# A second group of six gated tiles as block products in the down projection of a hybrid encoder trunk

## The chip, the core and the metric

The kernel runs as one program on one core of a Trainium2 chip. The metric is the device time of one execution in microseconds (us), given as the median of several runs; one further execution is taken by the hardware profiler, and every view in this document comes from such a profiled execution. TensorE (PE) multiplies matrices into PSUM, VectorE (DVE) and ScalarE (ACT) read PSUM and do arithmetic on SBUF, GpSimd (POOL) issues DMAs here that add to their destination in DRAM, and SyncE (SP) issues the plain loads.

## What is computed

Two layers of a streaming encoder on 1040 tokens (16 learned ones and 1024 of input) of width 1024. Each layer has an attention part, which the change leaves alone, and a gated feed-forward part with 2816 = 22 x 128 inner features:

```python
def conv_ffn(x, w_up, conv_w, conv_b, w_down):
    h = x @ w_up
    L = h.shape[1]
    hp = jnp.pad(h, ((0, 0), (CONV_W - 1, 0), (0, 0)))
    hc = conv_b
    for j in range(CONV_W):
        hc = hc + hp[:, j:j + L] * conv_w[j]
    u, g = jnp.split(hc, 2, axis=-1)
    return (jax.nn.silu(g) * u) @ w_down

for i in range(DEPTH):
    ...
    h = h + conv_ffn(rms_norm(h, ffn_norm[i]), w_up[i], conv_w[i], conv_b[i], w_down[i])
return rms_norm(h, final_norm)[:, N_META:]
```

The change concerns the last product, with `w_down`, and the addition to the residual `h`.

## The kernel before

**Layout.** Features lie on the 128 partitions and tokens along the free axis. The result of a layer's feed-forward part is 8 output tiles `m` of 128 features by 1040 tokens (1024 in the last layer, which drops the learned tokens). The 22 tiles that the down projection sums over are the gated tiles `j`, each 128 inner features. The tokens are worked in two halves of 520 (512 in the last layer), each in two matmul columns of 260 (256).

**Precision.** Every operand is split into a high and a low part (ACT casts, DVE subtracts: `weights`, `up_split`, `split`), and `mm3` (L253 to L255) multiplies high by high, low by high and high by low: three matmuls for each product of tiles.

**The order of the down projection.** `GROUPS` lists, per layer, groups of gated tiles as (kind, first tile, number of tiles); `LAST` holds the three last tiles. Before the change: three tiles of kind "n", eight of kind "s", two groups of four of kind "r", then `LAST`.

- Kinds "n" and "r" are plain (`plain` inside `ffn_down`): for each of the 8 output tiles and 2 halves, the group's tiles are accumulated in one of four PSUM places of two banks each. For "r", the residual tile `h` has been loaded from DRAM (`load_residual`, L1542) and DVE adds the PSUM sum onto it in SBUF (L1567). For "n", ACT copies the sum into one of three tiles `do` (L1569), and POOL issues a DMA that adds `do` to the residual in DRAM, `hm` (L1571).
- Kind "s" is done by seven block products in place of eight (`down_blocks`): the group's tiles are cut into two halves, output tiles are taken in pairs, and tokens in halves, which gives a two-by-two block product. Its left operands are sums and differences of weight blocks (`block_operand`, L1065 loads, L1075 combines), its right operands `X` are sums and differences of gated tiles. The four pairs are worked in a fixed order of products; the sums leave PSUM by copies (L1474) and adds (L1473) into tiles `du` and `dg`, which two accumulating DMAs for each pair add to `hm` (L1494, L1498).
- `LAST` is done by `down_last`, in column chunks of 400, 384 and 256 tokens (512, 256 and 256 in the last layer) over eight single PSUM banks. It adds the sum to the residual `h` in SBUF and feeds the next norm. Its weights stay in SBUF in tiles `wl`.

**The operands.** The gated tiles come back from DRAM (`actd`). `prepare` is one generator that goes through the groups in order and, step by step, loads tiles (L1365 for "s", L1359 for the others), splits plain tiles into `ah` and `al` and builds the operands of an "s" group: seven splits and four combinations (L1413) for each run of two tiles per half, or of one where the number is odd. Its steps are taken by `pump` at fixed points of the loops, as far as SBUF slots are free, and by `complete` where they are needed at once. SBUF slots of 1040 elements are lent out of one list, 39 of them in this stage; an "s" group of eight tiles holds 28 for its operands, and gives them back product by product while the last pair of output tiles is worked.

**What sets the order.** PE runs in the order of the program. The instructions of the other engines and queues are ordered by a planner, which takes the earliest instruction of the program that it thinks ready; each engine and each queue then works strictly in that order, so an instruction that waits holds up those behind it.

Of the kernel before, what the change touches and what calls it, by code (L numbers as in the profile page):

```python
# [46 lines left out]

GROUPS, LAST = (("n", 0, 3), ("s", 3, 8), ("r", 11, 4), ("r", 15, 4)), (19, 3)  # L50
HALVES, HALVES_LAST, HALVES_OUT = (0, 520, 520), (8, 524, 516), (16, 528, 512)
AHEAD = 4
FIRST_OPS = {2: 2, 7: 5}
# [1769 lines left out]
```

## Time and profile before

| | before |
|---|---|
| median of 3 runs | 2519.89 us (2518.92 to 2520.88) |
| profiled execution | 2519.71 us |
| its span | 2517.9 us |
| instructions | 48454 |
| granted TensorE clock, mean over the span | 0.997 |
| DMA | 258.25 MB, mean 103 GB/s |
| accumulating and other DMAs issued by POOL (q0) | 72.68 MB, 10.3% of the 16 engines' span |
| loads issued by SP (q1) | 181.74 MB, 23.2% |

The span is what the profile covers; 1.8 us of the execution lie around it. The down projection of layer 0 takes from 1017 to 1260 us of the span, that of layer 1 from 2263 us to the end, with the final norm. A view that groups instructions gives for each line, engine, operation and tile the shape, the count, the busy time and the mean of one in ns, and behind the bar the idle time of the engine just before them with what ended it. In a list by time each row begins with start and duration. An instruction "h<-down" writes h and reads down.

### The profile page before, as it was taken

To read this page: it belongs to the slowest core of one execution; us is meant where nothing else is said; L and a number is where in the kernel's file an instruction comes from. 1 tells how busy PE (TensorE), PEld (TensorE's weight loads), DVE (VectorE), ACT (ScalarE), POOL (GpSimd) and SP (SyncE) were. 2 spreads that over 40 slices of the span, in tenths; PEclk is the share of its full clock that TensorE was granted. 3 is DMA by queue.
4 is the path that set the end of the run, shared out by engine and by line. 5 is a ranking of instruction groups with operands and counts; after the bars stand their busy time and mean duration, and the time that the engine had idled before them with its cause. 6 is when DMAs were issued, how large, how long until landed. Compare 5 with 4: busy or idle time off the path is not lost.

```text
span 2517.9 us, 48454 instructions
## 1 busy us (share of the span) xinstructions
PE 2468.1 (98%) x19266; PEld 2410.1 (96%) x19266; DVE 1731.1 (69%) x3367; ACT 1283.1 (51%) x2604; POOL 405.6 (16%) x582
## 2 busy tenths in 40 slices
PE   8999999999999999999999999999999999999998
PEld 7989999899999999999999899999999999999997
DVE  7656766769877777853565666777697777787445
ACT  7336666656544455631353466665564444455312
POOL 4033333210000000100211334331100000001002
PEclk9999999999999999999999999999999999999999
DMA  3232134342322224863312222253432222257622
GB/s 123 64 95 63 50 96 131 115 140 72 118 81 81 81 77 132 204 164 115 103 55 70 74 75 77 65 154 109 136 93 92 85 77 80 80 164 176 197 62 77
DMA packets 116211, 258.25 MB, mean 103 GB/s; under 512 B 14624, under 2 KB 31296, under 8 KB 115984
## 3 DMA queue, kind: packets, MB, share of 16 engines
q1 hardware_dynamic: 92832, 181.74, 23.2%
q0 software_dynamic: 22432, 72.68, 10.3%
q8 instruction: 151, 2.47, 0.4%
q10 hardware_dynamic: 720, 0.74, 0.1%
q14 instruction: 76, 0.62, 0.1%
HBM read 174.50 MB, written 67.81 MB: 96 GB/s over the span
## 4 chain that ended last, share of the span: by engine, by line
PE 63%; issue 17%; DVE 12%; ACT 3%; DMA 3%; POOL 1%; SPq 0%; DVEq 0%; POOLq 0%; ACTq 0%
PE mm L253 7%; PE mm L255 7%; PE mm L254 7%; PE up L253 5%; PE up L255 5%; PE up L254 5%; PE down L254 4%; PE down L255 4%; PE down L253 4%; PE av L768 3%; PE tr L750 2%; PE S L714 1%; PE S L713 1%; PE wo L253 1%; PE wo L255 1%
## 5 line engine op out<-in xcount | busy, mean ns | idle before, releaser
L253 PE MATMUL up<-x,hi 128*128 128x260 f32 (+1 forms) x2464 | 697.4, 283 | 2.2 <-DVE hg L1295 1.3
L255 PE MATMUL up<-x,hi 128*128 128x260 f32 (+1 forms) x2464 | 695.5, 282 | 2.4 <-DVE x L1117 2.4
L254 PE MATMUL up<-x,lo 128*128 128x260 f32 (+1 forms) x2464 | 696.1, 283 | 0.3 <-DVE lo L1093 0.3
L255 PEld LDWEIGHTS up<-x,hi 128*128 128x128 f32 x2464 | 465.7, 189 | 3.2 <-DVE x L1117 3.2
L253 PEld LDWEIGHTS up<-x,hi 128*128 128x128 f32 x2464 | 464.6, 189 | 3.3 <-DVE hg L1295 1.8
L254 PEld LDWEIGHTS up<-x,lo 128*128 128x128 f32 x2464 | 464.9, 189 | 0.6 <-DVE lo L1093 0.5
L1093 DVE TENSOR_TENSOR lo<-raw,hi 128x512 fp32r<-128x512 f32 x364 | 247.9, 685 | 187.3 <-ACT hi L1092 179.6
L253 PE MATMUL mm<-xh,hi 128*128 128x348 f32 (+4 forms) x1056 | 362.6, 343 | 0.0
L255 PE MATMUL mm<-xl,hi 128*128 128x348 f32 (+4 forms) x1056 | 339.9, 322 | 0.0
L254 PE MATMUL mm<-xh,lo 128*128 128x348 f32 (+4 forms) x1056 | 338.9, 321 | 0.0
L1092 ACT CAST hi<-raw 128x512 fp32r<-128x512 f32 x364 | 224.5, 621 | 145.1 <-PE up L255 84.1
L253 PEld LDWEIGHTS mm<-xh,hi 128*128 128x128 f32 x1056 | 199.6, 189 | 5.8 <-issue 4.6
L254 PEld LDWEIGHTS mm<-xh,lo 128*128 128x128 f32 x1056 | 199.5, 189 | 0.6 <-issue 0.3
L255 PEld LDWEIGHTS mm<-xl,hi 128*128 128x128 f32 x1056 | 198.4, 188 | 0.6 <-issue 0.3
L253 PE MATMUL down<-ah,hi 128*128 128x260 f32 (+1 forms) x704 | 198.0, 281 | 0.8 <-DVE h L1567 0.8
L254 PE MATMUL down<-ah,lo 128*128 128x260 f32 (+1 forms) x704 | 198.2, 282 | 0.5 <-DVE lo L222 0.4
L255 PE MATMUL down<-al,hi 128*128 128x260 f32 (+1 forms) x704 | 198.4, 282 | 0.0
L379 DVE TENSOR_TENSOR PT<-tr,PT 116x464 fp32r<-116x464 f32 (+3 forms) x240 | 122.2, 515 | 68.9 <-ACT PT L378 67.1
L220 ACT CAST hi<-raw 128x512 fp32r<-128x512 f32 (+1 forms) x160 | 96.8, 607 | 128.7 <-PE down L255 95.1
L729 ACT ACTIVATE P<-P,m 116x924 f32<-116x924 f32 (+4 forms) x144 | 110.6, 768 | 72.1 <-DVE m L721 66.7
L1320 POOL DMA_DIRECT2D actd<-cv x44 | 23.6, 536 | 765.7 <-DVE cv L1319 744.7
L750 PE MATMUL tr<-ident,P 116*116 116x116 f32 x704 | 142.8, 267 | 0.8 <-DVE PT L379 0.5
(302 smaller groups left out, 5766.3 us busy)
## 6 DMA issues: line engine op xcount, KB each, us to landing
raw<-in_wm_dram SPq DMA_DIRECT2D x322, 256.0 KB, 2.8
raw<-in_wd_dram SPq DMA_DIRECT2D x64, 256.0 KB, 3.5
actd<-cv POOLq DMA_DIRECT2D x22, 520.0 KB, 3.0
actd<-cv POOLq DMA_DIRECT2D x22, 512.0 KB, 3.2
cb<-cd SPq DMA_DIRECT2D x16, 520.0 KB, 4.1
st<-actd SPq DMA_DIRECT2D x14, 520.0 KB, 4.6
st<-actd SPq DMA_DIRECT2D x14, 512.0 KB, 4.8
kA<-kA SPq DMA_DIRECT2D x24, 260.0 KB, 4.3
```

The costliest lines, as they stand in the source:

```text
L220: nc.scalar.copy(hi[:, :n, :], raw[:, :n, :])
L253: nc.tensor.matmul(ps, wh, xh[:, c0:c0 + n], start=first, stop=False, skip_group_check=more)
L254: nc.tensor.matmul(ps, wl, xh[:, c0:c0 + n], start=False, stop=False, skip_group_check=more)
L255: nc.tensor.matmul(ps, wh, xl[:, c0:c0 + n], start=False, stop=last, skip_group_check=more)
L379: nc.vector.tensor_tensor(out=lo, in0=src, in1=hi.bitcast(F32), op=ALU.subtract)
L713: nc.tensor.matmul(S[:rows, :n], q["qA"][e][:, qs], q["kA"][e][:, c0:k1], start=True, stop=False)
L714: nc.tensor.matmul(S[:rows, :n], q["qA"][e][:, qs], q["kL"][e][:, c0:k1], start=False, stop=True)
L729: nc.scalar.activation(x, x, AF.Exp, scale=-1.0, bias=low, accum_out=(den if nch < 3 else d2[:rows, 0:1]))
L750: nc.tensor.transpose(tr[:w, j, :rows], P[:rows, o:o + w], id_)
L768: nc.tensor.matmul(av[:, a:width], w.rearrange("p a b -> p (a b)"), x, start=(t == 0 and i == 0), stop=(t == last and i == 1))
L1092: nc.scalar.copy(hi[:, :nk, :], src[:, :nk, :])
L1093: nc.vector.tensor_tensor(out=lo[:, :nk, :], in0=src[:, :nk, :], in1=hi[:, :nk, :].bitcast(F32), op=ALU.subtract)
```

## The change

Behind the first "s" group, the two "r" groups of four gated tiles go. In their place come a plain group of kind "n" with two tiles (11 and 12) and a second "s" group with six tiles (13 to 18), three in each half. With no "r" group left, no sum is added to the residual in SBUF before `LAST`: all of them go to `hm` in DRAM by accumulating DMAs, and `load_residual()` at the end of `ffn_down`'s `run` loads all eight residual tiles, after the last group in program order. `prepare`, `down_blocks` and the dictionary `X` of operands follow the list. No line moves.

```diff
-GROUPS, LAST = (("n", 0, 3), ("s", 3, 8), ("r", 11, 4), ("r", 15, 4)), (19, 3)
+GROUPS, LAST = (("n", 0, 3), ("s", 3, 8), ("n", 11, 2), ("s", 13, 6)), (19, 3)
```

The functions that follow from it, in the lines that decide:

```python
for kind, g0, ng in GROUPS:
    if kind == "s":
        parts.append((g0, ng))
        continue
    ...
        if not isinstance(part, list):
            complete(lambda: built(part))
            blocks[1]()
            continue
...
load_residual()
complete(lambda: all(j in acts for j in range(LAST[0], sum(LAST))))
return hT
```

## The prediction

> **What bounds the kernel now.** I read the page's engine shares first, then its chain that ended last:
>
> ```profile
> PE 2468.1 (98%) x19266; PEld 2410.1 (96%) x19266; DVE 1731.1 (69%) x3367; ACT 1283.1 (51%) x2604; POOL 405.6 (16%) x582
> PE 63%; issue 17%; DVE 12%; ACT 3%; DMA 3%; POOL 1%; SPq 0%; DVEq 0%; POOLq 0%; ACTq 0%
> ```
>
> TensorE is busy for 98% of the span and leads the chain, so a matmul taken out can pay, if nothing else becomes late at its place. To read that place I took the time-ordered list of PE and looked for the instruction that opens each group of the down projection (layer 0 first, then layer 1):
>
> ```profile
> 1017.37 0.28 PE L253 MATMUL down<-ah,hi 128*128 128x260 f32 x1
> 1052.15 0.28 PE L253 MATMUL down<-x,hi 128*128 128x260 f32 x1
> 1134.42 0.28 PE L253 MATMUL down<-ah,hi 128*128 128x260 f32 x1
> 1226.25 0.34 PE L253 MATMUL mm<-ah,wl 128*128 128x400 f32 x1
> 1226.43 0.34 PE L254 MATMUL mm<-ah,wl 128*128 128x400 f32 x1
> 2379.30 0.28 PE L253 MATMUL down<-ah,hi 128*128 128x256 f32 x1
> 2471.29 0.39 PE L253 MATMUL mm<-ah,wl 128*128 128x512 f32 x1
> ```
>
> Layer 0: three plain tiles from 1017.37, the block group from 1052.15, the two plain groups that go straight into the residual ("r") from 1134.42, the last three tiles from 1226.25. The busy times of exactly these stretches (columns: length, PE, PEld, DVE, ACT, POOL, granted clock, DMA share, GB/s):
>
> ```profile
> 1017.37:1052.15 34.78, 34.70 (x290) 34.50 (x289) 33.06 (x38) 26.99 (x41) 6.56 (x8) 1.00 0.85 180
> 1134.42:1226.25 91.83, 91.83 (x770) 91.83 (x769) 35.56 (x53) 14.38 (x24) 1.69 (x2) 1.00 0.33 95
> 1226.25:1260.53 34.28, 34.28 (x220) 34.23 (x219) 26.61 (x46) 20.05 (x42) 17.43 (x17) 1.00 0.40 137
> 2379.30:2471.29 91.99, 91.20 (x770) 91.00 (x769) 34.49 (x51) 13.53 (x22) 1.69 (x2) 1.00 0.30 83
> ```
>
> The replaced "r" stretch is pure TensorE: no gap in layer 0, 0.8 us in layer 1, VectorE at 39%, ScalarE at 16%, clock 1.00. Nothing but matmuls is to be won there, and there is spare time on both evacuating engines.
>
> **What is removed.** By the loops a plain tile costs 8 output tiles x 2 halves x 2 columns x 3 = 96 matmuls. The 8 "r" tiles are 768 matmuls in 91.83 us: 0.1196 us each. After the change two plain tiles cost 192, and six as blocks cost 4 pairs x 7 products x 3 x 2 x 3 = 504: 696 together. Saved: 72 matmuls, 8.6 us a layer, **17.2 us** in two layers. The new plain group lasts 192 x 0.1196 = 23.0 us (2.87 a output tile), a block product 18 x 0.1196 = 2.15 us (24 x 0.1196 = 2.87 in the present group).
>
> **Arithmetic added on VectorE and ScalarE.** Groups by line and shape:
>
> ```profile
> L378 ACT CAST x<-st 128x1040 fp32r<-128x1040 f32 x9 | 9.4, 1066 | 4.1 <-DVE st L1413 3.1 <-DMA st<-actd 0.8
> L379 DVE TENSOR_TENSOR x<-st,x 128x1040 fp32r<-128x1040 f32 x9 | 10.9, 1235 | 1.3 <-ACT x L378 1.2
> L1569 ACT COPY do<-down 128x520 f32<-128x520 f32 x16 | 9.1, 591 | 0.0
> L1473 DVE TENSOR_TENSOR du<-down,du 128x520 f32<-128x520 f32 x8 | 5.6, 697 | 6.8 <-PE down L255 6.8
> L220 ACT CAST hi<-raw 128x384 fp32r<-128x384 f32 x6 | 3.1, 516 | 0.0
> L222 DVE TENSOR_TENSOR lo<-raw,hi 128x384 fp32r<-128x384 f32 x6 | 3.3, 550 | 0.0
> L235 ACT CAST both<-raw 128x256 fp32r<-128x256 f32 x1 | 0.4, 406 | 5.1 <-PE down L255 5.1
> L236 DVE TENSOR_TENSOR both<-raw,both 128x256 fp32r<-128x256 f32 x1 | 0.4, 414 | 0.0
> ```
>
> Per layer, the new operands are 7 splits and 4 combinations, once 1040 and once 520 wide: VectorE 11 x (1.235 + 0.697) = 21.3, ScalarE 7 x (1.066 + 0.591) = 11.6. The two plain tiles' splits: 2.5 and 2.1. Block weights (384 wide): VectorE 28 splits and 16 combinations x 0.550 = 24.2, ScalarE 28 x 0.516 = 14.4. Plain weights (256 wide) 8 x 0.41 = 3.3 on each. Block sums leave by 12 adds x 0.697 = 8.4 and 16 copies x 0.591 = 9.5, plain sums by 16 copies = 9.5. Together 59.7 on VectorE and 50.4 on ScalarE; what goes is less than the 35.56 and 14.38 above. The stretch is now 83.3 us of PE, and some of the operand work falls in the block group before it, so at most 72% and 61%: hidden behind the matmuls. The first plain stretch shows that this works even at 33.06 of 34.78 us on VectorE, with PE busy for 34.70. If that cover failed, the extra 24 us of VectorE a layer would show. The peak is the new plain group: ScalarE 9.5 + 3.3, two wide and seven narrow operand casts (6.3) and four block weights (2.1), 21.2 us in 23.0.
>
> The operands' order I followed through the code: the free slots let five of the seven pairs be built during the last pair of the first block group, as its own operands are given back, and the remainder during the first five plain output tiles. So the second block group finds them ready; bound, if not: the 520-wide half, 11 x 0.697 = 7.7 us a layer. I take 0 here.
>
> **Transfers and waits added.** Plain sums no longer meet the residual in SBUF; 16 accumulating DMAs a layer take them to DRAM.
>
> ```profile
> hm<-do POOLq DMA_DIRECT2D x8, 520.0 KB, 6.3
> h<-hm SPq DMA_DIRECT2D x8, 520.0 KB, 6.2
> raw<-in_wd_dram SPq DMA_DIRECT2D x32, 192.0 KB, 2.4
> q0 software_dynamic: 1148, 4.26, 65.5%
> DMA to landing us min/median/max: 5.2/6.0/10.0
> L1542 SPq EVENT_SEMAPHORE  x16: 17/28/8500, 1124.0 to 2389.1; - x16
> ```
>
> The fourth row is the queue in the 38 us from 1018: 65.5% of all engines for 4.26 MB, eight such DMAs, so 24.9 / 8 = 3.1 us of all sixteen each (the fifth is their time to landing; the last row's three figures are the shortest, median and longest wait of SP in ns).
>
> (a) New plain group: eight of them need 25 us of DMA in 23.0 us. There are three "do" tiles, so the copy of tile m+3 (ScalarE) waits for the landing of tile m: it is wanted 2 x 2.87 + 1.4 = 7.2 us after m ends, and landing takes 0.6 + 6.2 = 6.8. It just fits; at the longest landing, 10.0, it is 3.4 late. Behind a waiting copy on ScalarE stand weight and operand casts, and for these TensorE waits; four PSUM places cover some 4 us. Bounds 0 to 5 us a layer (the early plain group, with 4.3 us a tile, lost 0.1 in layer 0); I take **0.8**, near the row's median.
>
> The Trainium skill, "DMA: Bandwidth & Descriptors" (section Issuing engines are not separate DMA queues), says that all engines' DMAs share the same 16 DMA engines, which is against this change. The section Anatomy of one DMA fits 2.0 us + bytes / 436e3; estimated from it, 520 KB take 3.2 us, the copies would not wait and the sum would be 1.6 us better. The trace's 6.3 us disagrees with the fit for accumulating DMAs.
>
> (b) Blocks: the present block groups show what short products cost when an evacuation is late:
>
> ```profile
> PE down L253 <- ACT dg L1474: 1.0, 1, 1.0
> PE down L253 <- DVE dg L1473: 0.8, 1, 0.8
> PE down L253 <- DVE h L1567: 0.8, 1, 0.8
> PE down L253 <- DVE dg L1473: 0.2, 1, 0.2
> ```
>
> The first and fourth row stand in both layers, the second in layer 1: 1.2 and 2.0 us (28 products each). Another 28 products, each with 0.72 us less to hide an evacuation, beside lighter DMA: bounds 0 to 28 x 0.3 = 8; I take **1.6** a layer. The third row, 0.8 in layer 1, belongs to the removed adds and goes.
>
> (c) Residual loaded last: h6 and h7 can only be read when the last pair's two accumulates have landed, and these start when the last product ends (t0). Today the same chain stands ahead of 92 us of "r":
>
> ```profile
> 1134.59 0.85 POOL L1498 DMA_DIRECT2D hm<-du  x1 [17.14 <-DVE du L1473]
> 1135.51 0.84 POOL L1494 DMA_DIRECT2D hm<-dg  x1
> 1143.16 3.19 SPq L1542 DMA_DIRECT2D h<-hm  x2
> 1073.87 0.33 SPq L211 DMA_DIRECT2D raw<-in_wd_dram  x1
> ```
>
> SP stood for 8.5 us (its semaphore row above) and loaded h6 at 1143.2, 8.8 after the group's end; with 6.2 us of landing h6 comes at t0 + 15, h7 near t0 + 18. TensorE reaches output tiles 6 and 7 of its first column chunk at t0 + 10 and 12 (9 matmuls x 0.18 us a tile), and has eight banks: it goes on for 13 us without any evacuation. VectorE waits some 4 us, and at 26.61 of 34.28 us it has 7.7 to catch up. The last group's weights are issued on SP too, but the fourth row shows SP issuing weights 60 us before the plain group that they serve, so I expect them ahead of the waiting loads. Bounds 0 to 15 us; I take **0.8**.
>
> Sum: -17.2 - 0.8 + 2 x (0.8 + 1.6 + 0.8) = -11.6. The profiled execution took 2519.71 (span 2517.9 and 1.8 around it); 2508.1 follows, and beside the median 2519.89, 0.18 higher, **2508.3 us**.
>
> **The rivals.**
> 1. Waits nearly vanish (as in the "r" stretch): 2519.9 - 17.2 = 2502.7, or 2501 if present block waits shrink too. Against it: every block group so far lost over 1 us. 10%.
> 2. The new plain group is paced by DMA and the short products wait: (a) and (b) near their ends, 3 + 4 us a layer: 2519.9 - 18.0 + 14 = 2516. For it: 25 us of accumulates in 23.0 us, DMA share 0.85 already in the slower group. Against: the cover of four PSUM places. 17%.
> 3. Slower: the last group's weights stand behind the h6/h7 loads on SP. TensorE then stops at t0 until accumulate (8.8 after t0), weight landing (2.4) and both splits (1.1) are over: 12 us a layer, 2519.9 - 18.0 + 24 = 2526. It decides from the point where these waits pass 9 us a layer. For it: SP really did block in front of a row of weight loads. Against: the early issue shown above. 13%. The Trainium skill, "TensorE: Matmul & The Clock Gate" (section What's actually happening), adds that an idle window of about 3.4 us halves the clock; by it some 1.7 us more a stop. In the rows here the clock is 1.00 throughout, and no gap is that long.
> 4. The change is not what it says: the matmul count would stay 19266. Under 1%, in the forecast's share.
>
> **The numbers.** Forecast 60% (2503 to 2513), rivals as above. Without the worst of the third and the best of the first the range is 2501 to 2520. A measurement here tells 0.2%, 5 us, from no change. Faster by more: forecast, rival 1 and a quarter of rival 2, 0.74; within: most of rival 2 and a little of rival 3, 0.14; slower 0.12.
>
> **What would show it.** PE at 19122 matmuls; no "h<-down" adds; 64 "do" copies; 32 accumulates from "do" and 32 from "du"/"dg". The stretch from the first block group's end to the last group's first matmul near 85.7 us (83.3 + 2.4) where it was 91.8. Step (a) is wrong if ScalarE's copies wait on "hm<-do" and PE shows gaps there; (b) if PE's waits on "dg"/"du" in the second block group are far from 1.6; (c) if PE waits for "wl" or "h" after it. I would be wrong altogether if a weight load is issued late because SP waits.

## The result, and the profile after

The changed kernel takes **2545.28 us** (median of 4 runs, 2545.01 to 2548.13) against 2520.22 beside it: ratio 1.0103, 95% interval [1.0092, 1.0115]. It was forecast at 2508.3 in a range of 2501 to 2520, and is 37.0 us above the forecast and 25 us slower than before. The profiled execution took 2545.29 us with a span of 2543.5.

The engine shares, from the page of the changed kernel:

```profile
PE 2462.3 (97%) x19122; PEld 2399.8 (94%) x19122; DVE 1760.0 (69%) x3431; ACT 1337.3 (53%) x2724; POOL 432.0 (17%) x614
```

TensorE has the 144 matmuls less that were forecast, but its busy time fell by only 5.8 us and the span grew by 25.6: it stands still for about 81 us in all, 49.8 before. The stretches of the down projection show where (columns as before: length, PE, PEld, DVE, ACT, POOL, granted clock, DMA share, GB/s):

```profile
1053.73:1137.86 84.13, 80.80 (x674) 80.59 (x673) 46.42 (x66) 31.46 (x52) 6.31 (x8) 1.00 0.60 149
1137.86:1171.10 33.24, 26.54 (x194) 25.71 (x193) 17.55 (x30) 17.76 (x34) 7.20 (x9) 0.90 0.82 173
1171.10:1234.65 63.55, 60.91 (x507) 60.49 (x505) 27.20 (x47) 22.29 (x44) 6.93 (x9) 1.00 0.66 151
1234.65:1277.81 43.16, 37.13 (x217) 35.65 (x218) 30.60 (x53) 23.68 (x51) 18.65 (x19) 0.96 0.71 217
2397.34:2431.37 34.03, 25.93 (x195) 24.88 (x194) 17.94 (x31) 18.20 (x35) 7.60 (x9) 0.90 0.81 170
2431.37:2493.40 62.03, 60.07 (x507) 59.55 (x505) 26.98 (x47) 22.17 (x44) 6.93 (x9) 1.00 0.67 151
```

The rows are, for layer 0, the first block group, the new plain group of two tiles, the new block group of six and the last group; for layer 1 the two new ones. Against before:

| stretch (us) | before, layer 0 / 1 | after, layer 0 / 1 | forecast |
|---|---|---|---|
| first plain group | 34.8 / 34.3 | 34.9 / 34.5 | as before |
| first block group | 82.3 / 82.2 | 84.1 / 83.2 | as before |
| new plain group | - | 33.2 / 34.0 | 23.0, with (a) 23.8 |
| new block group | - | 63.6 / 62.0 | 60.3, with (b) 61.9 |
| both, or "r" before | 91.8 / 92.0 | 96.8 / 96.1 | 85.7 |
| last group, to the next layer's first matmul; in layer 1 to the end of the span | 34.1 / 46.6 | 43.2 / 50.1 | 0.8 more |

Above the forecast stand 11.1 + 10.4 in the two new groups, 1.9 + 1.0 in the first block group and 8.3 + 2.7 in the last: 35.4 of 37.0. Most of the remainder is 1.5 us by which the down projection already began later in this execution; that start lay between 1016.1 and 1020.0 in the kernels of this study, so it tells nothing.

The waits of PE, by what released it (total us, times, longest), in layer 0 and, below, three rows from layer 1:

```profile
PE mm L253 <- ACT wl L220: 6.7, 3, 3.9
PE down L254 <- DVE lo L222: 5.3, 2, 5.1
PE down L253 <- ACT du L1474: 3.3, 1, 3.3
PE down L253 <- ACT do L1569: 3.1, 3, 1.5
```

```profile
PE down L254 <- DVE lo L222: 6.2, 2, 5.9
PE down L253 <- ACT du L1474: 3.2, 1, 3.2
PE mm L253 <- ACT wl L220: 2.6, 2, 1.5
```

Three of the four rows of layer 0 were not in the sum: the split of the plain group's own weights (L222), a copy in the *first* block group (L1474), and the last group's weights (L220). For the first, the DMA view of the changed kernel between 1134 and 1172 (KB each, median us to landing):

```profile
hm<-do POOLq DMA_DIRECT2D x7, 520.0 KB, 8.4
raw<-in_wd_dram SPq DMA_DIRECT2D x7, 192.0 KB, 5.9
```

The block weights, 192 KB each in this group, land in 5.9 us; loads of that size landed in 2.4 in the kernel before. The chain of the changed kernel shows what follows, and below it the 10 us windows:

```profile
1149.54 9.12 DMA raw<-in_wd_dram
1159.15 0.55 DVE raw L1075
1159.71 0.35 DVE lo L222
1160.10 0.58 PE down L254
```

```profile
1150.00:1160.00 10.00, 4.42 (x33) 3.80 (x31) 3.22 (x7) 4.62 (x9) 1.69 (x2) 0.93 1.06 231
1160.00:1170.00 10.00, 9.90 (x62) 9.90 (x63) 5.03 (x12) 5.03 (x11) 2.32 (x3) 0.73 0.52 115
```

The DMA engines are full (share 1.06). A block weight takes 9.1 us; VectorE's combination of it (L1075) waits, and behind it, in VectorE's order, the split that the plain group's next matmul needs. TensorE stands still for 5 us, and then runs at a granted clock of 0.73 in the ten us that follow.

The chain at the wait in the first block group:

```profile
1098.07 7.92 DMA hm<-du
1106.08 1.25 DVE al L379
1107.41 1.06 ACT ah L378
1108.47 0.50 ACT du L1474
1109.02 0.39 PE down L253
```

An accumulating DMA still reads a "du" tile; its slot has been given to `al` of the *next* plain group, so the subtraction that writes `al` waits, the next cast on ScalarE waits for that, and a copy out of PSUM stands behind the cast.

At the last group, SP's list by time, and below it ScalarE's:

```profile
1225.60 7.59 SPq L1542 DMA_DIRECT2D h<-hm  x2
1235.21 0.33 SPq L211 DMA_DIRECT2D raw<-in_wd_dram  x1
1240.05 3.33 SPq L1542 DMA_DIRECT2D h<-hm  x3
1243.48 1.33 SPq L211 DMA_DIRECT2D raw<-in_wd_dram  x3
```

```profile
1233.59 0.59 ACT L1474 COPY dg<-down 128x520 f32<-128x520 f32 x1 [5.88 <-PE down L255]
1234.08 1.75 ACT L220 CAST wl<-raw 128x384 fp32r<-128x384 f32 x4
1243.05 0.51 ACT L220 CAST wl<-raw 128x384 fp32r<-128x384 f32 x1 [4.80 <-DMA raw<-in_wd_dram]
```

Here rival 3 seems confirmed: weights five to eight are issued behind loads of the residual. But the first four were there: their casts run without a pause, and they begin only at 1234.08, as the block group ends. Something other than SP held them.

### The profile page after: what moved, and what is told of

Same layout as the page of the kernel before. It is cut to its first block, busy times and chain, and to the rows that moved or that the text cites. A ratio compares the mean times of both kernels' runs of the same rounds, so it can differ in the third digit from the quotient of the medians.

```text
span 2543.5 us, 48519 instructions
## 1 busy us (share of the span) xinstructions
PE 2462.3 (97%) x19122; PEld 2399.8 (94%) x19122; DVE 1760.0 (69%) x3431; ACT 1337.3 (53%) x2724; POOL 432.0 (17%) x614
## 4 chain that ended last, share of the span: by engine, by line
PE 75%; DVE 12%; DMA 5%; issue 4%; ACT 3%; POOL 1%; SPq 0%; DVEq 0%; ACTq 0%; POOLq 0%
PE up L253 10%; PE up L254 10%; PE up L255 10%; PE mm L253 7%; PE mm L255 7%; PE mm L254 7%; PE down L253 3%; PE down L254 3%; PE down L255 3%; PE av L768 3%; PE tr L750 2%; DMA raw<-in_wd_dram 1%; PE S L713 1%; PE S L714 1%; DMA hm<-dg 1%
## 5 line engine op out<-in xcount | busy, mean ns | idle before, releaser
L1093 DVE TENSOR_TENSOR lo<-raw,hi 128x512 fp32r<-128x512 f32 (+1 forms) x420 | 278.5, 668 | 214.7 <-ACT hi L1092 207.0
L1092 ACT CAST hi<-raw 128x512 fp32r<-128x512 f32 (+1 forms) x420 | 252.7, 606 | 176.1 <-PE up L255 84.5
L253 PE MATMUL down<-x,hi 128*128 128x260 f32 (+1 forms) x784 | 221.5, 282 | 8.9 <-ACT du L1474 6.5
L255 PE MATMUL down<-x,hi 128*128 128x260 f32 (+1 forms) x784 | 221.0, 282 | 0.0
L254 PE MATMUL down<-x,lo 128*128 128x260 f32 (+1 forms) x784 | 220.6, 281 | 0.0
L1075 DVE TENSOR_TENSOR raw<-raw,raw 128x512 f32<-128x512 f32 (+1 forms) x230 | 146.8, 666 | 35.8 <-DMA raw<-in_wd_dram 31.3
L253 PEld LDWEIGHTS down<-x,hi 128*128 128x128 f32 x784 | 147.6, 188 | 10.1 <-ACT du L1474 6.9
```

Source lines behind the costliest of these rows:

```text
L253: nc.tensor.matmul(ps, wh, xh[:, c0:c0 + n], start=first, stop=False, skip_group_check=more)
L254: nc.tensor.matmul(ps, wl, xh[:, c0:c0 + n], start=False, stop=False, skip_group_check=more)
L255: nc.tensor.matmul(ps, wh, xl[:, c0:c0 + n], start=False, stop=last, skip_group_check=more)
L1075: nc.vector.tensor_tensor(out=q[out][:, :nk, :], in0=q[a][:, :nk, :], in1=q[b][:, :nk, :], op=op)
L1092: nc.scalar.copy(hi[:, :nk, :], src[:, :nk, :])
L1093: nc.vector.tensor_tensor(out=lo[:, :nk, :], in0=src[:, :nk, :], in1=hi[:, :nk, :].bitcast(F32), op=ALU.subtract)
```

## The experiments

Five theories, by letters:

- **S** (rival 3): the last group's weights wait on SP behind the residual's loads.
- **M**: the `wl` tiles lie on memory that the block group's weights occupy to its last product. The first four casts wait for that, hold all four `raw` tiles, and so the other four loads come late as well.
- **D**: the accumulates of the middle plain group need 25 us of all DMA engines, which a group of 23 us cannot hide.
- **Q**: the slot wait in the first block group.
- **L**: the residual, loaded last, makes ScalarE and VectorE late, which shows at the head of layer 1.

Every kernel was timed in three rounds against the kernel before (pair_half in five), whose medians lay between 2518.5 and 2519.24.

| kernel | median us | ratio to before, 95% interval |
|---|---|---|
| h_pool | 2556.02 | 1.0144 [1.0129, 1.0159] |
| pair_w | 2542.00 | 1.0088 [1.0069, 1.0106] |
| h_pool_pair | 2542.11 | 1.0096 [1.0079, 1.0112] |
| no_acc | 2528.52 | 1.0037 [1.0024, 1.0050] |
| wl_early | 2539.79 | 1.0082 [1.0067, 1.0097] |
| pair_wl | 2531.22 | 1.0047 [1.0031, 1.0064] |
| mid3 | 2548.09 | 1.0122 [1.0097, 1.0147] |
| mid3_wl | 2542.45 | 1.0093 [1.0077, 1.0108] |
| swap_wl | 2529.35 | 1.0041 [1.0026, 1.0056] |
| resid | 2549.41 | 1.0118 [1.0103, 1.0133] |
| pair_wl_do5 | 2536.86 | 1.0071 [1.0052, 1.0091] |
| all | 2542.43 | 1.0091 [1.0076, 1.0106] |
| mid3_s4 | 2535.27 | 1.0069 [1.0054, 1.0084] |
| mid4_s4 | 2530.82 | 1.0054 [1.0037, 1.0070] |
| pair_swap_wl | 2521.44 | 1.0014 [1.0005, 1.0023] |
| no_acc_swap_wl | 2515.98 | 0.9990 [0.9981, 0.9999] |
| pair_half | 2532.98 | 1.0055 [1.0042, 1.0068] |
| no_acc_half | 2517.34 | 0.9997 [0.9987, 1.0006] |

### The last group: S or M

**h_pool**: POOL issues the residual's loads, so that nothing of them stands on SP.

```diff
-                nc.sync.dma_start(hT[k][:, o0:T], self.hm[k][:, o0:T])
+                nc.gpsimd.dma_start(hT[k][:, o0:T], self.hm[k][:, o0:T])
```

> The changed kernel with one edit: the eight residual loads are issued by POOL instead of SP. Theory S (the last group's weights stand on SP behind residual loads that wait for accumulating DMAs): TensorE's waits for wl go (6.7 us in layer 0, 2.6 in layer 1, and the slow clock behind them), the last group's stretch in layer 0 falls from 43.2 to 35 to 37 us, the whole to 2532 to 2537 us. Rival R (the late residual itself stops TensorE, since sums stay in PSUM until it is there): no change within 2 us, 2543 to 2547.

Measured: 2556.02 us, 11 more than the change. PE's waits in this kernel, around the last group of layer 0 and of layer 1:

```profile
PE mm L253 <- ACT wl L220: 7.0, 3, 3.3
```

```profile
PE ssq L364 <- POOL r L355: 3.3, 1, 3.3
```

The last group of layer 0 falls from 43.2 to 39.2 us, so the order on SP may have a share. But waits for `wl` are still there (the longest, 3.3, is one at the head of layer 1, the other 3.7 lie in the last group), the stretch to layer 1's down projection grows from 1001.8 to 1006.4 us, and in layer 1 TensorE waits for POOL's own work for the norm. S alone is refuted. **h_pool_pair**, the same with the edit of pair_w below, gained nothing over pair_w either.

> Both edits together: residual loads by POOL and paired weights in the two-tile plain group. If S and W hold, the gains add up: 2517 to 2524 us; if R and D hold, 2540 to 2546; one of the two alone gives 2530 to 2537.

**wl_early**: the first four `wl` tiles go into ordinary slots, the last four onto the block weights' memory as before.

```diff
-                pair = [s.get(F32R, "wl", (128, 2, 4, 128), es) for _ in range(2)]
+                pair = [s.get(F32R, "wl", (128, 2, 4, 128), es if m >= KD // 2 else ()) for _ in range(2)]
```

> The changed kernel with one edit: the first four output tiles' weights of the last group take general slots, and the second four take the slots that lie on the block weights' memory (before: the other way round). Theory M (the first four cannot be written until the last block product has read its weights, they hold the four raw tiles, and the second four are loaded late): TensorE's waits for wl go, the last group's stretch falls from 43.2 to 35 to 37 us in layer 0 and by 3 to 4 us in layer 1, the whole to 2532 to 2537 us. Rival C (the DMA engines are full of residual loads and accumulates at that place, so the weights land late whatever their tiles): a gain of at most 4 us, 2541 to 2546.

The last group of layer 0 in this kernel, and PE's wait just behind it:

```profile
1236.24:1270.39 34.15, 34.15 (x219) 34.14 (x217) 22.99 (x40) 19.83 (x41) 15.72 (x15) 1.00 0.79 238
```

```profile
PE mm L253 <- ACT wl L220: 4.3, 1, 4.3
```

34.15 us, as before the change and without a gap: **M is shown**. But of the 9.0 us only part is kept. From the last group's end to layer 1's down projection it takes 1008.84 us, 1002.49 before the change and 1001.84 with it, so that 7.0 of the 9.0 us are lost again there. The wait in the second row is for weights of the next layer, whose cast stands on ScalarE behind the norm's work, and ScalarE and VectorE are late with that. This is what L has foreseen; its cause follows below.

### The new plain group: D

**pair_w**: weights of two output tiles in one load, one cast and one split, in groups of two tiles.

```diff
+                if ng == 2:
+                    ahead.extend(self.weights_pair(self.wd[lyr, m:m + 2, :, g0:g0 + 2, :]))
+                    return
                 ahead.append(self.weights(self.wd[lyr, m][:, g0:g0 + ng, :]))
```

> The changed kernel with one edit: the weights of the two-tile plain group are loaded, cast and split for two output tiles at a time (one raw, one hi and one lo tile for two). Theory W (the second block group's first weights are asked for late, because the plain group's small loads occupy the four raw tiles one by one): TensorE's wait of 5 to 6 us for lo in the plain group goes, its stretch falls from 33 to 25 to 27 us, the whole to 2530 to 2535. Rival D (the accumulating DMAs saturate the DMA engines, and everything lands late): the stretch stays over 30 us, the whole 2540 to 2546.

The group falls from 33.2 to 26.3 us and the wait for L222 is gone; waits of about 1 us for "do" copies stay, and the block group behind it grows by some 2.5 us. Of 7 us a layer, 3.3 in all reach the end, and the four runs lie as far apart as 2534.9 and 2547.0. **pair_wl** joins it with wl_early and is 8.6 us below wl_early.

> Paired weights in the two-tile group and the slots of wl_early together: if M holds, 10 us under paired weights alone, 2529 to 2534; under C 2538 to 2542.

**no_acc**: the eight accumulating DMAs of the middle plain group are left out, so that its sums are missing from the result.

```diff
-            if kind == "n":
+            if kind == "n" and g0 == 0:
                 nc.gpsimd.dma_start(self.hm[m][:, o0:T], out[:, o0:T], accum_op=ALU.add)
```

> The changed kernel without the eight accumulating DMAs of the two-tile plain group in each layer (its sums are left out of the result). Theory D: the stretch of the plain group falls from 33 to about 24 us and the whole by 17 to 21 us, to 2524 to 2528. Theory W: only the copies' waits for do tiles go (about 3 us a layer), the wait for lo stays; the whole 2537 to 2541.

2528.52 us, **17 less than the change**. Its plain group in layer 0, and the landing of block weights there:

```profile
1137.68:1162.24 24.56, 23.54 (x194) 23.12 (x193) 18.67 (x31) 18.52 (x36) 1.16 (x2) 1.00 0.59 146
```

```profile
raw<-in_wd_dram SPq DMA_DIRECT2D x9, 192.0 KB, 2.4
```

Without the accumulates block weights land in 2.4 us again and the group takes 24.56, though ScalarE and VectorE do the same work. In layer 1 it takes 27.0, with a wait of 1.8 us for a "do" copy and a granted clock of 0.66 in the five us behind it. The arithmetic was nearly hidden, as forecast; the transfers were not.

**mid3**: the rounds are exchanged: two tiles plain, six as blocks, three plain, eight as blocks.

```diff
-GROUPS, LAST = (("n", 0, 3), ("s", 3, 8), ("n", 11, 2), ("s", 13, 6)), (19, 3)
+GROUPS, LAST = (("n", 0, 2), ("s", 2, 6), ("n", 8, 3), ("s", 11, 8)), (19, 3)
```

> The same 22 tiles with the two rounds exchanged: two plain and six as blocks first, then three plain and eight as blocks, so the same 1656 matmuls a layer before the last group. Theory D (eight accumulating DMAs do not fit behind 23 us of matmuls, but do behind 34.5): the middle group loses under 2 us a layer, the first group now loses some (it has two tiles, but less other traffic), the whole 2527 to 2533 with the last group's waits unchanged. Rival O (the operands of the second block group are what comes late): eight tiles need a third more of them, the middle group loses as much or more, 2543 to 2555.

Its six-tile block group and the plain group of three behind it, in layer 0:

```profile
1050.80:1122.30 71.50, 64.32 (x507) 63.50 (x505) 39.43 (x61) 28.40 (x52) 7.66 (x9) 0.95 0.74 186
1122.30:1156.70 34.40, 34.40 (x290) 34.40 (x289) 25.59 (x31) 22.72 (x36) 6.81 (x8) 1.00 0.94 200
```

With three tiles the same eight accumulates hide behind 34.4 us without a gap, at a DMA share of 0.94. The short group, now the first, takes 33.8 and 28.7 us where its matmuls take 23, and hands its transfers on to the block group behind it (71.5). So three edits each take most of the group's loss away: fewer loads, no accumulates, a longer group. **That the accumulates bring the loss is shown**, by no_acc above all. D as it is worded is not the whole of it: with all eight accumulates in place, a group of two tiles takes 26.3 us with paired weights, and 26.3 in layer 1 of swap_wl below. That is 3.3 us above its 23.0; the other 7 of the change come where a load that lands late holds up the group's own split. Since the short group of mid3 is only moved, the time doesn't fall; the 2527 to 2533 expected were missed. **mid3_wl** adds wl_early: its last group takes 34.2 us, and 46.9 to the end of the span in layer 1, as before the change, and the kernel is again far above the 2515 to 2522 expected.

> mid3 with the slots of wl_early: under D and M 2515 to 2522; under D alone 2526 to 2532; under O and C over 2540.

### The first block group: Q

**swap_wl**: wl_early, and in `prepare` the later plain groups take their `ah` and `al` slots before the next tile is fetched.

```diff
-                    fetch()
+                    if not g0:
+                        fetch()
                     t = use()
                     ah, al = s.get(F32R, "ah"), s.get(F32R, "al")
+                    if g0:
+                        fetch()
```

> wl_early with one edit: when a plain tile of the middle or last group is split, its two operand slots are taken before the next load's slots and not behind them. Theory Q (in the last pair of the first block group a split waits for a slot that an accumulating DMA still reads, and on ScalarE the copy out of PSUM stands behind it): the gap of 3 to 3.7 us before the next product goes, and the slow clock behind it; the first block group falls from 85.5 to 82 to 83 us, the whole by 5 to 8 us from 2539.8, to 2532 to 2535. Rival (the copy is late for another reason, such as the load): no change within 2 us.

2529.35 us, 10.4 below wl_early. Its first block group in layer 0:

```profile
1053.26:1133.80 80.54, 80.54 (x675) 80.54 (x674) 44.33 (x62) 31.38 (x51) 5.91 (x7) 1.00 0.61 153
```

The wait is gone, and these 80.54 us have no gap: **Q is shown**. In layer 1 the wait for "du" is gone as well, and one of 1.9 us for "dg" stands in that group (82.8 us). The new plain group still takes 33.5 in layer 0, where TensorE now waits 4.6 us for a "do" copy. In layer 1 it takes 26.3, with all accumulates in place and the DMA engines at a share of 0.99:

```profile
2390.23:2416.53 26.30, 24.02 (x193) 23.39 (x193) 15.66 (x27) 16.85 (x32) 5.92 (x7) 0.99 0.99 210
```

So the gain is not Q's alone: between the profiled executions of wl_early and swap_wl 7.7 us go in the two first block groups and 8.5 in this plain group, and some is lost behind them. Why the edit helps this group in layer 1 only, no run takes apart.

### Cures that only moved the wait

**pair_wl_do5**: pair_wl with five "do" tiles in place of three in the middle group.

```diff
-                going.extend(s.get(F32, "do") for _ in range(3))
+                going.extend(s.get(F32, "do") for _ in range(5 if g0 else 3))
```

> pair_wl with five do tiles in place of three in the middle group. If what is left there is the copies' waits for do tiles (four of 0.5 to 1 us and one of 2.3 a layer), both stretches fall by 4 to 6 us a layer together, 2520 to 2524 from 2531.2. If the DMA backlog delays the weights too, no more than 2 us a layer, 2527 to 2531.

The plain group gains 1 us a layer; the block group behind it gets waits of 4.6 and 5.2 us for copies into "du", and the kernel is 5.6 us above pair_wl. That the two more "do" tiles hold the slots which "du" wants is my reading; it wasn't tried apart.

**resid**: wl_early, and the second block group's sums are added by VectorE onto a residual loaded beforehand, without accumulates or reload.

```diff
+            if res:
+                return onto(j, p)
...
+        def residual(m):
+            load_residual(m + 4)
+            return hT[m]
```

> wl_early with one edit: the second block group adds its sums with VectorE onto the residual, loaded beforehand, so its eight accumulating DMAs and the reload behind them go. Theory L (the residual that comes late is what the next layer's first products wait for, since the norm and its weights' casts stand behind it): the 4.7 and 0.9 us gaps at the head of layer 1 go, with the slow clock behind them, 6 us in all, 2532 to 2535. Rival (they come from the weights' order): no change, and VectorE's 16 more adds a layer may cost 1 to 3 us, 2540 to 2543.

The stretch to layer 1's down projection falls to 1002.8 us, so L is right about the place. But, with `load_residual` looking four tiles ahead, the residual's loads wait on the middle group's accumulates, and PE's waits in the two new groups of layer 0 are these:

```profile
PE down L253 <- ACT do L1595: 9.9, 4, 5.4
PE down L253 <- DVE h L1473: 5.6, 2, 4.1
```

**all** joins pair, five "do" tiles, wl_early, swap and resid: 2542.43. It has the same two waits, 9.1 and 6.0 us in layer 0.

> All edits together: paired weights, five do tiles, the slots of wl_early, the split's slots first, the second block group onto the residual. If the four causes are those named and add up, the stretches come to 83 + 24 + 61 us beside 82 + 92 before: 2505 to 2512, faster than both kernels. If one of them only moves the wait, 2512 to 2522.

### Do the causes add up?

**pair_swap_wl** is swap_wl and pair_w together, the change as it is with three cures.

> The change as it is with all three cures that helped one by one: weights of two output tiles in one load, the last group's weights out of busy memory, slots before the fetch. If the cures add up (2531 less some 5 us of the slot wait), 2524 to 2528 us; if the wait only moves on to the copies of the outputs, 2530 to 2537.

2521.44 us, below the 2524 to 2528 expected: the cures add up, and 24 of the 37 us are back with every transfer in place. It is the fastest version with all sums, and still not faster than before.

**no_acc_swap_wl** is swap_wl without the middle group's accumulates, whose sums are missing.

> The same cures without the pair, and the middle plain group's eight accumulating transfers left out, so that its sums are missing from the result. If the named causes are the whole loss, the time is that of before less most of the 17.2 us of matmuls, plus up to 6 us at the head of the second layer: 2506 to 2514 us. Over 2518 would show a cost that no named cause holds.

2515.98, just above what was expected if these causes were all. The groups of layer 0 ahead of the last one now take 5.1 us less than before the change; but the stretch to layer 1's down projection takes 1009.56 us, the price that wl_early had shown. ScalarE's longest wait for data in the last group of layer 0 tells why, with the DMA view of 1220 to 1235:

```profile
ACT both L235 <- DMA raw<-in_wm_dram: 5.1, 1, 5.1
```

```profile
raw<-in_wm_dram SPq DMA_DIRECT2D x1, 256.0 KB, 8.1
```

The next layer's first weight takes 8.1 us to land, where the page of the changed kernel has a median of 2.8 for such loads: the block group's last accumulates and the reloads of the residual fill the DMA engines at that time. Its cast stands in ScalarE's order amid the last group's work, and VectorE waits behind it for as long.

**pair_half** (on top of pair_swap_wl) and **no_acc_half** (on top of no_acc_swap_wl, so that its middle sums are missing) try to remove that: only the last two pairs of output tiles are added onto a residual that is loaded early.

```diff
+            if res and (j, p) == (1, 2):
+                res(KD - 1)
+            if res and j >= NP // 2:
+                return onto(j, p)
```

> The three cures of the run before it, and the residual of the last four output tiles loaded early, while the second block group computes its second pair: the last two pairs of block products are added onto it by VectorE and need neither an accumulating transfer nor a reload. If the residual's lateness (the last reloads land 12 us into the last group, and VectorE is still behind at the head of the second layer) is what is left of the loss, the head of the second layer loses its 6 us of gaps, the end some 2 us, and the time is 2511 to 2515 us, below before. If the early loads only move the wait into the block group, as they did when all eight tiles were loaded early, it is 2520 us or more.

> The same residual edit with the middle plain group's eight accumulating transfers left out (its sums are missing from the result) and without the pair. All named causes are then away at once: the time should be that of before less most of the 17.2 us of matmuls, 2504 to 2509 us. If it stays at 2512 or more, a cost is left that no named cause holds.

The stretch from the last group's end to layer 1's down projection, in no_acc_swap_wl:

```profile
1254.94:2264.50 1009.56, 994.31 (x7684) 970.17 (x7683) 723.59 (x1485) 541.79 (x1136) 165.55 (x250) 0.99 0.29 92
```

and in no_acc_half, with ScalarE's list by time in its second block group:

```profile
1261.25:2263.25 1002.00, 990.64 (x7684) 966.23 (x7683) 718.06 (x1475) 537.14 (x1127) 161.40 (x247) 1.00 0.29 92
```

```profile
1185.58 0.51 ACT L220 CAST wl<-raw 128x384 fp32r<-128x384 f32 x1 [5.48 <-DMA hm<-dg]
1186.00 0.58 ACT L1490 COPY du<-down 128x520 f32<-128x520 f32 x1
```

The head of layer 1 is whole again (1002.00), and VectorE's wait for that weight is gone, so **L's price of 7 us is shown**. But nothing is gained, and the 2504 to 2509 us expected with all named causes away were missed: the last group's `wl` got a slot that an accumulate of "dg" was still reading, and a PSUM copy stood behind that cast, for which TensorE waited 2.8 us. That it got this slot because the residual's four early tiles had taken others is my reading. The block group takes 67.3 us where it took 62.3. With the accumulates (pair_half) it takes 72.5, and the kernel loses 11.5 us to pair_swap_wl.

**mid3_s4** and **mid4_s4** are swap_wl with a middle plain group of three or four tiles, a block group of four, and a last group of four or three; 48 matmuls a layer fewer than before.

```diff
-GROUPS, LAST = (("n", 0, 3), ("s", 3, 8), ("n", 11, 2), ("s", 13, 6)), (19, 3)
+GROUPS, LAST = (("n", 0, 3), ("s", 3, 8), ("n", 11, 3), ("s", 14, 4)), (18, 4)
...
+GROUPS, LAST = (("n", 0, 3), ("s", 3, 8), ("n", 11, 4), ("s", 15, 4)), (19, 3)
```

> Middle plain group of three gated tiles, block group of four, last group of four; the last group's first four weights out of the block weights' memory and the slots of the first block group taken before its next fetch. 48 matmuls a layer fewer than before, 11.5 us of TensorE. If the four named causes (accumulates that outlast a short group, the last group's weights in busy memory, the slot wait of the first block group, the residual loaded late) are all there is, the middle plain group takes 34 to 35 us without a wait of its own, the block group of four 40 to 42 us, and the time is 2508 to 2514 us, below before. If a further cost comes with any second block group, the time stays above 2518.

> The same with a middle plain group of four tiles (about 46 us) and a last group of three, which leaves as much time as before behind the reloads. The same 11.5 us of TensorE saved. If the pace of the accumulates is the cause, four tiles cover them with 20 us to spare and the time is 2510 to 2516 us; the late residual leaves up to 6 us at the head of the second layer. If a longer group is no help, over 2520.

Both missed: 2535.27 and 2530.82. The plain and the block group of mid4_s4 in layer 0:

```profile
1134.71:1180.53 45.82, 45.82 (x386) 45.82 (x385) 13.68 (x22) 16.31 (x29) 7.62 (x9) 1.00 0.74 147
1180.53:1229.10 48.57, 43.04 (x339) 42.11 (x337) 23.59 (x49) 19.73 (x44) 6.17 (x8) 0.96 0.67 154
```

Four tiles hide the accumulates completely, which D had said. The three of mid3_s4 do not: they take 38.0 and 38.1 us, with a wait of 2 us for a "do" copy each, where the three of mid3 took 34.4 and 33.9. So the length of the group does not settle it by itself. In mid4_s4 the 336 matmuls of the block group, 40.2 us at 0.1196, take 48.57: products of two tiles a half last 1.4 us, and TensorE waits for the evacuations of "du", "dg" and "do" for 5.5 us. That is the cost of step (b), at a size of group where it bites.

## Why the prediction was wrong

**Removed matmuls: right.** 19122 matmuls, 0.12 us each where nothing waits; the six-tile block group takes 60.9 and 60.1 us of busy PE against 60.3 forecast.

**Arithmetic hidden: right, nearly.** In layer 0 VectorE is busy for 44.8 and ScalarE for 40.1 of the two new groups' 96.8 us. Without the accumulates (no_acc) the plain group stands 1.6 us above its 23.0 in layer 0, and 4.0 in layer 1, where one copy is late and the clock falls behind it.

**Step (a) failed, by its size and its place.** Taken at 0.8 us a layer with a bound of 5, it cost 10.2 (33.24 less 23.0) and 11.0. The sum had the right warning, 25 us of DMA in 23.0, and then asked only whether the "do" copies would wait. Those wait for 3 us a layer. The larger part came to the other users of the same DMA engines: block weights land late, VectorE waits for one, and the plain group's own split stands behind it. No bound was made for that. The kernel before had shown it: the DMA view of its first plain group (1018 to 1056), from which the 65.5% in the prediction come, has this row, and the page gives 3.5 us as the median of all 64 loads of that size.

```profile
raw<-in_wd_dram SPq DMA_DIRECT2D x8, 256.0 KB, 5.5
```

The Trainium skill's "DMA: Bandwidth & Descriptors" (section Issuing engines are not separate DMA queues), cited then as speaking against the change, was the better guide: 192 KB take 5.9 us beside the accumulates and 2.4 without them. Rival 2 had this mechanism at 3 us a layer.

**Step (b) was too dear.** 1.6 us a layer were taken for its own short products; there its only wait of more than 0.4 us a layer is for a "do" copy of the group before (1.5 and 0.9). That the group's length (63.6 and 62.0) comes near the 61.9 of the sum is luck. The cost becomes large with two tiles a half (mid4_s4).

**The operands, taken at 0, failed.** They were ready in time, but loading their tiles early takes slots, four at a fetch, ahead of the plain tile's `ah` and `al`. So `al` got a slot that an accumulate of "du" was still reading, and the subtraction that waits for it holds up VectorE's and ScalarE's order: 3.3 and 3.2 us in the *first* block group, where the prediction saw no change. swap_wl, which exchanges these two steps, removes both waits.

**Step (c) failed.** Taken at 0.8 with bounds of 0 to 15, it cost 9.1 in layer 0 (43.2 less 34.1) and 3.5 in layer 1. Rival 3 named the place and the sign, but its mechanism, SP's order, is not the cause by itself (h_pool); the memory on which `wl` lies is (wl_early). "I expect them ahead of the waiting loads" was true of the first four loads, and of no use, since their casts had nowhere to write. Behind this wait a second price was hidden, the late residual's 7 us at the head of layer 1: again a weight that lands late beside accumulates, and work of two engines behind it.

**The clock.** The Trainium skill's "TensorE: Matmul & The Clock Gate" (section What's actually happening) has an idle window of about 3.4 us halve the clock, which the prediction used for rival 3 alone. Windows of the changed kernel (the columns as above) behind stops of 3.6, 5.5 and 4.2 us, measured from the start of one matmul to the next, and below them one of no_acc behind a stop of 2.1 us:

```profile
1110.00:1115.00 5.00, 5.00 (x45) 5.00 (x44) 3.36 (x6) 1.12 (x3) 0.00 (x0) 1.00 0.22 53
1160.00:1164.00 4.00, 3.90 (x18) 3.90 (x19) 0.84 (x3) 0.00 (x0) 0.00 (x0) 0.50 0.71 186
1250.30:1254.00 3.70, 3.61 (x12) 3.61 (x13) 3.70 (x6) 1.65 (x4) 2.08 (x2) 0.57 0.73 247
```

```profile
2397.00:2402.00 5.00, 5.00 (x31) 5.00 (x31) 5.00 (x9) 5.00 (x10) 0.00 (x0) 0.66 0.56 172
```

For the longer stops the trace agrees: the second and third left the clock at half for 5.3 and 3.4 us, so they cost some 2.7 and 1.7 us more than themselves, and a wait of 5 us counts as more than 7. For shorter ones it does not: the stop of 3.6 left the clock at 1.00, and that of 2.1 was followed by half the clock for 3.4 us. In the traces of this study every stop over 3.7 us in and behind the first down projection was followed by half the clock, and of the shorter ones from 2 us some were, so no threshold comes out of them.

**What the cause is.** One reading covers M, Q and the runs that moved the wait, though no run tests it as a whole: the "r" stretch of 92 us asked little of the slots and of the DMA engines, and all that was late from the block group before it caught up there. The change took out 8.6 us of matmuls and with them that rest. **What stays open**: with the cures and without the accumulates 2516 to 2517 us remain, 8 to 9 above the forecast. Most of it is L or what replaces it; whether some division of the slots is free of both was not found. That the lag at the head of layer 1 is due to the late residual is shown by the length of that stretch in resid and in the two runs with half of it loaded early; that it goes through the late weight is read from the waits, and no run loaded that weight earlier by itself.

## What to carry to other kernels

A stretch in which TensorE never waits may be where transfers and memory of its neighbours recover; before shortening it, add up what its DMA engines and free slots do for the stages on both sides. When transfers need more time on all DMA engines than the group that issues them lasts, price the landing of every other load in that stretch and what stands behind its consumer in program order, not only the tiles of those transfers. For each tile that is to be loaded early, look up on whose memory it lies and who reads that last.

## What was not expected of the hardware

Eight accumulating DMAs of 520 KB in a group of 33 us took the DMA share to 1.06 at 231 GB/s over ten of these us, and the median landing of the 192 KB loads beside them from 2.4 to 5.9 us, the longest on the chain 9.1. Leaving them out was worth 17 us, two thirds of what the change lost against before.
